# First weight tiles row by row through one queue, a position-bias table copied by ScalarE, and weights split four halves ahead

## The chip, the cores and the metric

The kernel runs on one core of one Trainium2 chip. The metric is the device time of one execution in microseconds (us), as the median of several runs.

The names used below: PE is TensorE (matmuls), ACT is ScalarE, DVE is VectorE, POOL is GpSimd, SP is SyncE, which here only issues DMAs. All weights and inputs are float32. A float32 operand is split into a part `hi`, rounded to the matmul format float32r, and the rest `lo`; a product is made from three matmuls (`hi*hi`, `hi*lo`, `lo*hi`, function `mm3`).

## The reference

A trunk of two layers over 256 positions and 2048 channels:

```python
h = x
for i in range(DEPTH):                       # DEPTH = 2
    hn = _rmsnorm(h, norm_g[i])
    u = hn @ w_in[i]                         # 2048 -> 5632 columns
    a_val, a_glu, a_z, q, k, v, b_z = jnp.split(u, offs, axis=-1)
    ya = _conformer_conv(a_val, a_glu, ...)  # GLU, depthwise conv of width 31, LayerNorm, SiLU
    ya = ya * jax.nn.silu(a_z)
    yb = _window_attention(q, k, v, bias_band, sink[i]) * jax.nn.silu(b_z)
    h = h + jnp.concatenate([ya, yb], axis=-1) @ w_out[i]
    e = _rmsnorm(p[i] @ w_pe[i], pe_g[i])
    h = h + e * jax.nn.sigmoid(h @ w_pg[i])
return _rmsnorm(h, final_g)
```

`bias_band` is a table of relative positions: for each head and each distance from -255 to 255 it holds `rel_bias[bucket(distance), head]`, or a very negative number beyond a distance of 128.

## The kernel before, in words

Everything is held transposed: channels on the 128 partitions, positions along the row. `x` is 16 slices (k = 0 to 15) of 128 channels by 256 positions. The weights lie in HBM as one stream in the order of use. Its unit is a *half*, 128x1024 numbers (512 KB), and two halves are a *chunk* of 1 MB, which is what one DMA normally brings (function `load`, line 166) into one of three buffers `raw`. ACT casts a half to `hi` (line 179) and DVE subtracts to get `lo` (line 180), both into one of five buffers `w`; this is `split`. `ahead(h)` splits up to half h, and `get(h)`, called when PE is to use half h, calls `ahead` first. PE, ACT and DVE work in the order of the program text (they are under a manual schedule); SP and POOL as the scheduler placed them. A row in a trace like `w<-raw` is such a cast or subtraction.

A HW DMA takes one of eight semaphores in turn, so the ninth waits for the first to have landed.

**The start.** Seven matmuls on zeros (`warm`, line 274) come first on PE. Then the first two of the eight column tiles of the GLU (value and gate each, so four 128-column groups) are computed from `x` that is not yet normalised, since the factor per position can be applied to the result: `firsts`, two PSUM banks, 16 slices x 4 groups x 3 matmuls = 192 matmuls named `ag`. For every slice ACT and DVE make `hg` (hi and lo of x times the gain, lines 563 and 564), ACT squares x (line 572, 8 operations of two slices), and DVE adds the squares into `sqs[0]` (lines 574 and 590). A half holds eight slices of one column group, and only the first 512 columns of four halves are needed for the first four slices; so the loads are cut into 256 KB parts (`load_part`, line 293), three of them issued by ACT and the rest by SP, and the work goes in four steps of four slices: split four parts, then 48 matmuls.

**The position embedding's product.** Then come four halves of `w_pe` (q = 0 to 3): `e = p @ w_pe`, 24 matmuls for each q in two groups of 12 (`epair`), whose results ACT copies out (line 519). Between them stands the norm's root: after q = 0, at the start of q = 1, PE sums the squares over partitions (`rh0c`, line 397), DVE makes the mean (`rh0v`, line 407), POOL takes the power -1/2 (`rh0col`, line 409), and PE turns the column into a row (`rh0b`, lines 416 and 418). ACT copies that row (line 422) and DVE scales the two banks of `firsts` by it (`ev`, line 600). The bank goes on to the sigmoid (`u`, line 637), the product (`az`) and the convolution on DVE (`cz`, line 623).

In before, `get(h)` for the first twelve halves of layer 0 splits two halves ahead of PE; from half 12 on it is `LS` = 4.

**The bias table.** `bias_prep` multiplies a one-hot table (33x511) by `rel_bias` on PE (`fps`, line 372), DVE copies the result (line 374) and POOL writes it to `fscr` in HBM. The attention reads its bands from there (`load_bias`).

After this the two layers go through their other tiles; the change leaves the code of those stages as it is.

Of the kernel before, what the change touches and what calls it, by code (L numbers as in the profile page):

```python
# [79 lines left out]
def weight_halves(l):  # L80
# [53 lines left out]

@with_exitstack
def trunk_kernel(ctx: ExitStack, tc: tile.TileContext, xT, pT, wst, par, gain, relb, sinkp, onehot, out):
# [24 lines left out]
    raws, spl, alone = {}, {}, {}  # L161
# [10 lines left out]
    def split_part(h, c):  # L172

        if h not in spl:
            w = wspl.tile([P, 2 * HALF + 64], F32R, tag="w", name=f"w{h}")
            spl[h] = w[:, SHIFT:SHIFT + 2 * HALF].rearrange("p (t n) -> p t n", t=2)
        raw = raws[h // 2][:, h % 2, c] if h // 2 in raws else alone[h][:, c]
        hi, lo = spl[h][:, 0, c], spl[h][:, 1, c]
        nc.scalar.copy(hi, raw)  # L179
        nc.vector.tensor_sub(lo, raw, hi.bitcast(F32))  # L180
# [100 lines left out]
    def load_part(h, n, eng=nc.sync, parts=2):  # L281

        c, x = h // 2, h % 2
        if h >= 6:
            if h not in alone:
                alone[h] = wk.tile([P, 4 * S + 32], F32, name=f"raw{h}alone", tag=f"qq{h % 2}", bufs=1)
            d = alone[h]
        else:
            if c not in raws:
                raws[c] = wraw.tile([P, 2, HALF], F32, tag="raw", name=f"raw{c}")  # L290
            d = raws[c][:, x, :]
        w = HALF // parts
        eng.dma_start(d[:, n * w:(n + 1) * w], wst[c, :, x * HALF + n * w:x * HALF + (n + 1) * w])

    def load_x(k, n=4, eng=nc.sync):
        eng.dma_start(h[k // 8][:, k % 8:k % 8 + n, :], xT[:, k:k + n, :])
# [6 lines left out]
    load_x(0, 1)  # L303
    nc.scalar.dma_start(gains, gain)
    load_x(1, 1)
    load_part(0, 0, nc.scalar)
    load_x(2, 2)
    load_part(1, 0, nc.scalar)
    load_part(2, 0, nc.scalar)
    junk = wk.tile([P, 2], F32, name="junk", tag="rv1", bufs=1)  # L310
    nc.scalar.activation(junk[:, 0:1], zeros[:, 0:1], AF.Copy, scale=2.0)
    load_part(3, 0)
    load_x(4)
    for x in range(4):
# [24 lines left out]
    relt = cst.tile([NUM_BUCKETS + 1, NQ], F32, name="relt")  # L339
    nc.vector.memset(relt[NUM_BUCKETS:NUM_BUCKETS + 1, :], NEG)  # L340
    oh = wk.tile([NUM_BUCKETS + 1, NREL], F32, name="oh", tag="sq", bufs=3)
    sinkt = cst.tile([P, DEPTH * NQ], F32, name="sinkt")

    def small_loads():
# [3 lines left out]
        nc.sync.dma_start(pf, pT[0])  # L348
        state["raw"] = 4
# [3 lines left out]
    def later_loads():  # L353

        for t in (oh[:, 0:1], sinkt[:, 0:1]):
            nc.vector.memset(t, 0.0)
        nc.sync.dma_start(relt[0:NUM_BUCKETS, :], relb)
        nc.sync.dma_start(oh, onehot)
# [10 lines left out]
    def bias_prep():  # L369
        nc.vector.tensor_scalar(nsink, sinkt, -1.0, None, ALU.mult)  # L370
        b = bank("fps").rearrange("p a b -> p (a b)")
        nc.tensor.matmul(b[0:NQ, 0:NREL], relt, oh, start=True, stop=True)
# [114 lines left out]
    for l in range(DEPTH):  # L487
# [65 lines left out]
        else:  # L553
            hg = [bigt(f"hg{l}_{i}", F32R) for i in range(2)]
            firsts = [bank(f"ag{l}_{t}") for t in range(2)]
            for n in range(4):
                c = slice((n % 2) * (HALF // 2), (n % 2 + 1) * (HALF // 2))
                ks = range(4 * n, 4 * n + 4)
                def part(k):

                    i, kk = k // 8, k % 8
                    hi, lo = (x[:, kk, :] for x in halves(hg[i]))
                    nc.scalar.activation(hi, h[i][:, kk, :], AF.Copy, scale=gcol(l, k))
                    nc.vector.scalar_tensor_tensor(lo, h[i][:, kk, :], gcol(l, k), hi.bitcast(F32),  # L564
                                                   ALU.mult, ALU.subtract)

                for y in range(4):
                    for k in ks[:1] if y == 0 else ks[1:] if y == 1 else []:
                        part(k)
                    split_part(4 * (n // 2) + y, c)  # L570
                for k in ks[::2]:
                    nc.scalar.activation(sqs[k // 2], h[k // 8][:, k % 8:k % 8 + 2, :], AF.Square)
                if n:
                    nc.vector.tensor_add(sqs[0], sqs[0], sqs[n])
                if n == 1:
                    small_loads()
                for y in range(4):
                    w = spl[4 * (n // 2) + y].rearrange("p t (k c) -> p t k c", k=8)
                    for k in ks:
                        mm3(firsts[y // 2][:, y % 2, :], w[:, :, k % 8, :], hg[k // 8][:, :, k % 8, :],  # L580
                            y % 2 == 0 and k == 0, k == KT - 1)
            for y in range(8):
                spl.pop(y)
# [4 lines left out]
            ahead(8)  # L588
            for x in range(4, 8):
                nc.vector.tensor_add(sqs[0], sqs[0], sqs[x])  # L590
            ahead(9)
# [60 lines left out]
        if l == 0:  # L652
            e = halves(bigt(f"e{l}"))
            eacc = wk.tile([P, 2, S], F32, name="eacc", tag="hacc")
            for q in range(4):
# [5 lines left out]
                if q == 2:  # L661
                    scaled = rstd_row(rcol, f"rh{l}", settle=2)
                    for t in range(2):
                        glu(t, firsts[t])
                for jj in range(0, 4, 2):
                    copied(4 * q + jj, epair(w, jj, pp))
                pump()

        def embed(l=l, eacc=eacc, e=e):

            if l == 0:
                yield from wait(4)
                bias_prep()
# [349 lines left out]
def buckets():  # L1023

    rel = np.arange(-(S - 1), S)
    half = NUM_BUCKETS // 2
    ret = (rel > 0).astype(np.int32) * half
    n = np.abs(rel)
    max_exact = half // 2
    large = max_exact + (np.log(np.maximum(n, 1) / max_exact) / np.log(MAX_DISTANCE / max_exact)  # L1030
                         * (half - max_exact)).astype(np.int32)
    large = np.minimum(large, half - 1)
    return ret + np.where(n < max_exact, n, large), n <= WINDOW


def band_onehot():
    b, band = buckets()
    m = np.zeros((NUM_BUCKETS + 1, NREL), np.float32)
    m[np.where(band, b, NUM_BUCKETS), np.arange(NREL)] = -1.0
    return np.ascontiguousarray(m[:, ::-1])  # L1040


# [5 lines left out]
def pack(inputs):  # L1048
# [17 lines left out]
    for l in range(DEPTH):  # L1066
# [31 lines left out]
```

## Time and profile before

| | |
|---|---|
| median of 3 runs | 932.85 us (932.72 to 933.32) |
| the profiled execution | 932.91 us; span from the first to the last instruction 931.1 us |
| PE busy | 920.1 us, 99% of the span |
| DVE busy | 773.9 us, 83% |
| ACT busy | 558.0 us, 60% |
| chain that ended last | PE 97%, ACT 1%, DVE 1%, DMA 1% |
| DMA | 182.55 MB, mean 196 GB/s |

A matmul's end is modelled in the profile, so two matmuls overlap in the rows, and a PE that is "busy" can still have lost a tenth of a microsecond between two starts. The time that PE lost is seen better in the distance from the start of one stage to the start of the next, compared with the number of matmuls between.

### The profile page before, as it was taken

The page shows a single profiled execution, that of the slowest core. Times are in us where ns is not written, and L with a number is a line of the kernel's source. Part 1 is how long each engine was busy: PE and PEld are TensorE (multiplying, and loading weights), DVE is VectorE, ACT ScalarE, POOL GpSimd, SP SyncE. Part 2 cuts the span into 40 slices and gives each one's busy share as a digit, 9 for nine tenths or more (in the row PEclk, how much of TensorE's full clock was granted, in tenths as well). Part 3 has the DMA queues.
Part 4 walks back from the last instruction along what each step waited for, and adds up shares of the span by engine and source line. Part 5 has one row for each costly group of instructions (what it writes and reads, how often), then busy time and mean ns, then how long its engine had stood idle before and what let it go on. Part 6 is the DMA issues. An engine that isn't in the chain of part 4 may idle for free.

```text
span 931.1 us, 19288 instructions
## 1 busy us (share of the span) xinstructions
PE 920.1 (99%) x8002; PEld 908.5 (98%) x8002; DVE 773.9 (83%) x1326; ACT 558.0 (60%) x853; POOL 59.4 (6%) x65
## 2 busy tenths in 40 slices
PE   9999999999999999999999999999999999999995
PEld 8999999999999999999999999999999999999995
DVE  7699999998998697786779998999888968777663
ACT  8744455688875475544466445568777556445551
POOL 0000101001000000011100000100100000000111
PEclk9999999999999999999999999999999999999998
DMA  9576546646455555556556555466454554655532
GB/s 338 204 250 222 188 176 207 209 167 206 170 193 220 182 226 181 182 184 260 190 185 224 187 221 182 182 221 215 157 178 170 198 210 152 234 184 182 207 108 90
DMA packets 30452, 182.55 MB, mean 196 GB/s; under 512 B 3756, under 2 KB 4573, under 8 KB 10653
## 3 DMA queue, kind: packets, MB, share of 16 engines
q1 hardware_dynamic: 25724, 166.46, 49.8%
q0 software_dynamic: 3344, 12.88, 4.1%
q10 hardware_dynamic: 1296, 1.99, 0.6%
q8 instruction: 62, 1.02, 0.4%
q14 instruction: 26, 0.20, 0.1%
HBM read 177.09 MB, written 4.23 MB: 195 GB/s over the span
## 4 chain that ended last, share of the span: by engine, by line
PE 97%; ACT 1%; DVE 1%; DMA 1%; issue 0%; SPq 0%; DVEq 0%; ACTq 0%
PE o L449 6%; PE o L450 6%; PE o L451 6%; PE g L451 6%; PE g L450 6%; PE g L449 6%; PE ag L451 6%; PE ag L450 6%; PE ag L449 6%; PE za L449 3%; PE za L450 3%; PE q L449 3%; PE za L451 3%; PE q L450 3%; PE q L451 3%; PE zb L449 3%
## 5 line engine op out<-in xcount | busy, mean ns | idle before, releaser
L180 DVE TENSOR_TENSOR w<-raw,w 128x1024 fp32r<-128x1024 f32 (+1 forms) x316 | 377.6, 1203 | 106.1 <-ACT w L179 104.9
L179 ACT CAST w<-raw 128x1024 fp32r<-128x1024 f32 (+1 forms) x316 | 319.0, 1030 | 178.2 <-PE o L451 38.8
L623 DVE SCALAR_TENSOR_TENSOR cz<-az,pars,cz 128x241 f32<-128x241 f32 (+14 forms) x480 | 202.9, 474 | 1.0 <-ACT cz L616 0.3
L451 PE MATMUL ag<-hg,w 128*128 128x256 f32 x512 | 141.6, 276 | 0.2 <-DVE w L180 0.2
L449 PE MATMUL ag<-hg,w 128*128 128x256 f32 x512 | 141.7, 277 | 0.0
L450 PE MATMUL ag<-hg,w 128*128 128x256 f32 x512 | 141.5, 276 | 0.1
L451 PE MATMUL g<-h,w 128*128 128x256 f32 x512 | 141.3, 276 | 0.0
L449 PE MATMUL g<-h,w 128*128 128x256 f32 x512 | 141.3, 276 | 0.0
L450 PE MATMUL g<-h,w 128*128 128x256 f32 x512 | 141.3, 276 | 0.0
L449 PEld LDWEIGHTS ag<-hg,w 128*128 128x128 f32 x512 | 96.1, 188 | 0.9 <-issue 0.8
L451 PEld LDWEIGHTS ag<-hg,w 128*128 128x128 f32 x512 | 96.1, 188 | 0.6 <-DVE w L180 0.6
L450 PEld LDWEIGHTS ag<-hg,w 128*128 128x128 f32 x512 | 96.1, 188 | 0.4 <-DVE hg L564 0.3
L449 PEld LDWEIGHTS g<-h,w 128*128 128x128 f32 x512 | 96.1, 188 | 0.0
L450 PEld LDWEIGHTS g<-h,w 128*128 128x128 f32 x512 | 96.1, 188 | 0.0
L451 PEld LDWEIGHTS g<-h,w 128*128 128x128 f32 x512 | 96.1, 188 | 0.0
L449 PE MATMUL o<-yb,w 128*128 128x256 f32 x256 | 71.8, 280 | 0.0
L449 PE MATMUL za<-hg,w 128*128 128x256 f32 x256 | 71.7, 280 | 0.0
L449 PE MATMUL q<-hg,w 128*128 128x256 f32 x256 | 71.4, 279 | 0.0
L449 PE MATMUL zb<-hg,w 128*128 128x256 f32 x256 | 71.3, 278 | 0.0
L450 PE MATMUL o<-yb,w 128*128 128x256 f32 x256 | 71.1, 278 | 0.0
L451 PE MATMUL o<-yb,w 128*128 128x256 f32 x256 | 71.1, 278 | 0.0
L451 PE MATMUL za<-hg,w 128*128 128x256 f32 x256 | 71.0, 277 | 0.0
(249 smaller groups left out, 2286.0 us busy)
## 6 DMA issues: line engine op xcount, KB each, us to landing
raw<-in_wst SPq DMA_DIRECT2D x152, 1024.0 KB, 4.8
bias<-fscr POOLq DMA_DIRECT2D x16, 384.0 KB, 3.9
raw<-in_wst SPq DMA_DIRECT2D x9, 256.0 KB, 7.0
az<-in_xT POOLq DMA_DIRECT2D x4, 512.0 KB, 5.3
hscr<-e POOLq DMA_DIRECT2D x2, 1024.0 KB, 6.7
az<-hscr POOLq DMA_DIRECT2D x4, 512.0 KB, 6.4
x<-in_xT SPq DMA_DIRECT2D x3, 512.0 KB, 6.8
out_t<-og ACTq DMA_DIRECT2D x4, 256.0 KB, 3.7
```

What stands on the lines that cost most here:

```text
L179: nc.scalar.copy(hi, raw)
L180: nc.vector.tensor_sub(lo, raw, hi.bitcast(F32))
L449: nc.tensor.matmul(o, w[:, 0], x[:, 0], start=start, stop=False, skip_group_check=True)
L450: nc.tensor.matmul(o, w[:, 0], x[:, 1], start=False, stop=False, skip_group_check=True)
L451: nc.tensor.matmul(o, w[:, 1], x[:, 0], start=False, stop=stop, skip_group_check=True)
L623: nc.vector.scalar_tensor_tensor(acc[:, t, lo_:hi_], a[:, t, lo_ + s:hi_ + s], w(k), acc[:, t, lo_:hi_], ALU.mult, ALU.add)
```

## The change

It has four parts, all in layer 0 before the first tile of normalised input:

1. **Rows.** The first eight halves hold two slices of all four column groups each, instead of eight slices of one. A quarter of a chunk (256 KB, a *row*) is what one slice needs. The loads (`load_rows`) and those of x go through SP alone, x and rows in turn; the last four rows come as one 1 MB DMA behind `p`, into the buffer that rows 0 to 3 had. The work goes in eight steps of two slices: operands, split, squares of the step before, 24 matmuls.
2. **Further ahead.** `get(h)` splits four halves ahead from the start; the halves of `w_pe` are then split earlier, and so are the first ones of tile 2. The norm's root row `rh0b` and what follows from it stand in the middle of q = 1, not at the end.
3. **The bias's table.** The one-hot, its load and the matmul go. `relb` is loaded transposed (16 heads on partitions, 32 buckets) by POOL at the start; the 511 places of the table are 33 runs of one bucket, two of them beyond the band. ACT writes 31 runs (`fs`, each a bucket's column broadcast, times -1), DVE sets the two others; two runs for each pump of the side work.
4. **Sigmoid first.** The first operation of ACT (`junk`) is a Sigmoid, not a Copy, so that its table is loaded at the start.

```diff
-    for ts in FIRST_TILES:
+    if l == 0:
+        cols = np.concatenate([off + tile_cols(t) for t in range(2) for off in (OFF_VAL, OFF_GLU)])
+        out += [("w_in", cols, k, 2) for k in range(0, KT, 2)] + W_PE
+    for ts in FIRST_TILES[l == 0:]:
...
+def bias_runs():
+    b, band = buckets()
+    v = [int(x) if y else None for x, y in zip(b[::-1], band[::-1])]
+    at = [n for n in range(NREL) if n == 0 or v[n] != v[n - 1]] + [NREL]
+    return [(x, y, v[x]) for x, y in zip(at, at[1:])]
...
     def get(h):
         r = h - NHALF
-        if h < 12:
-            ahead(h + 2)
-        elif 0 <= r < 12:
+        if 0 <= r < 12:
             ahead(h + (r | 1) + 2 - r)
         else:
             ahead(h + LS)
...
+    def load_rows(k, n=1):
+        c, w = k // 4, 2 * HALF // 4
+        if c not in raws:
+            raws[c] = wraw.tile([P, 2, HALF], F32, tag="raw", name=f"raw{c}")
+        x = (k % 4) * w
+        nc.sync.dma_start(raws[c].rearrange("p a b -> p (a b)")[:, x:x + n * w], wst[c, :, x:x + n * w])
...
+    for k in range(2):
+        load_x(k, 1)
+        load_rows(k)
+    for k in (2, 4, 6):
+        load_x(k, 2)
+        load_rows(k)
+        load_rows(k + 1)
+    load_x(8)
+    load_rows(8, 2)
+    load_rows(10, 2)
+    load_x(12)
     junk = wk.tile([P, 2], F32, name="junk", tag="rv1", bufs=1)
-    nc.scalar.activation(junk[:, 0:1], zeros[:, 0:1], AF.Copy, scale=2.0)
+    nc.scalar.activation(junk[:, 0:1], zeros[:, 0:1], AF.Sigmoid)
...
         nc.sync.dma_start(pf, pT[0])
+        load_rows(12, 4)
         state["raw"] = 4
         load(4)
...
     def bias_prep():
         nc.vector.tensor_scalar(nsink, sinkt, -1.0, None, ALU.mult)
-        b = bank("fps").rearrange("p a b -> p (a b)")
-        nc.tensor.matmul(b[0:NQ, 0:NREL], relt, oh, start=True, stop=True)
-        fs = wk.tile([NQ, NREL], F32, name="fs", tag="sq", bufs=3)
-        nc.vector.tensor_copy(fs, b[0:NQ, 0:NREL])
+        fs = wk.tile([P, 4 * S + 32], F32, name="fs", tag="qq0", bufs=1)[0:NQ, 0:NREL]
+        for n, (a, b, c) in enumerate(BIAS_RUNS):
+            if c is None:
+                nc.vector.memset(fs[:, a:b], -NEG)
+            else:
+                nc.scalar.mul(fs[:, a:b], relt[:, c:c + 1].broadcast_to([NQ, b - a]), -1.0)
+            if n % 2:
+                yield
...
+            for k in range(0, KT, 2):
+                part(k)
+                if k < 8:
+                    split_part(k // 2, slice(0, HALF // 2))
+                    part(k + 1)
+                    split_part(k // 2, slice(HALF // 2, HALF))
+                else:
+                    part(k + 1)
+                    split(k // 2)
+                if k:
+                    squares(k // 2 - 1)
+                if k == 4:
+                    small_loads()
+                w = spl.pop(k // 2).rearrange("p t (k y c) -> p t k y c", k=2, y=4)
+                for x in range(2):
+                    for y in range(4):
+                        mm3(firsts[y // 2][:, y % 2, :], w[:, :, x, y, :], hg[k // 8][:, :, (k + x) % 8, :], ...)
+            squares(7)
...
-            ahead(8)
-            for x in range(4, 8):
+            ahead(9)
+            for x in (1, 3, 5, 7):
                 nc.vector.tensor_add(sqs[0], sqs[0], sqs[x])
-            ahead(9)
+            ahead(10)
...
                 w = get(n).rearrange("p t (j k c) -> p t j k c", j=4, k=2)
-                if q == 2:
-                    scaled = rstd_row(rcol, f"rh{l}", settle=2)
-                    for t in range(2):
-                        glu(t, firsts[t])
                 for jj in range(0, 4, 2):
+                    if q == 1 and jj:
+                        scaled = rstd_row(rcol, f"rh{l}", settle=2)
+                        for t in range(2):
+                            glu(t, firsts[t])
                     copied(4 * q + jj, epair(w, jj, pp))
...
             if l == 0:
-                yield from wait(4)
-                bias_prep()
+                yield from bias_prep()
```

How the instructions stand shows three places. The first is DVE's queue around the norm's mean `rh0v`. In both, `w` is the subtraction of a half, `sqx` x4 are the last four sums of squares, `pp` is the lo part of p. Before:

```order
L484 TENSOR_TENSOR pp<-p_111,pp 128x512
L180 TENSOR_TENSOR w_463<-raw_267,w_463 128x1024
L590 TENSOR_TENSOR sqx<-sqx 128x512 x4
L180 TENSOR_TENSOR w_470<-raw_267,w_470 128x1024
L356 MEMSET oh 33x1
L356 MEMSET sinkt 128x1
L180 TENSOR_TENSOR w_485<-raw_459,w_485 128x1024
L407 TENSOR_SCALAR rh0v<-rh0c 128x2
L180 TENSOR_TENSOR w_525<-raw_459,w_525 128x1024
```

Now (line numbers of the changed kernel):

```order
L500 TENSOR_TENSOR pp<-p_111,pp 128x512
L205 TENSOR_TENSOR w_451<-raw_251,w_451 128x1024
L205 TENSOR_TENSOR w_454<-raw_251,w_454 128x1024
L612 TENSOR_TENSOR sqx<-sqx 128x512 x4
L205 TENSOR_TENSOR w_463<-raw_447,w_463 128x1024
L369 MEMSET sinkt 128x1
L205 TENSOR_TENSOR w_473<-raw_447,w_473 128x1024
L205 TENSOR_TENSOR w_478<-raw_449,w_478 128x1024
L423 TENSOR_SCALAR rh0v<-rh0c 128x2
L205 TENSOR_TENSOR w_518<-raw_449,w_518 128x1024
```

Five subtractions of whole halves stand ahead of `rh0v` where there were three, and two of them stand ahead of the sums of squares where there was one. The four rows of `w_pe` and the first half of tile 2 (`w_478`) are among them.

The second place is PE's queue around the root's row `rh0b`; `e` are the products of `w_pe`. Before, between the second group of q = 1 (`w_470`) and the first of q = 2:

```order
L451 MATMUL e<-pp,w_470 128x256
L416 MATMUL rh0b<-ident,rh0col 128x128 x2
L418 MATMUL rh0b<-ones 128x1 x2
L449 MATMUL e<-pp,w_485 128x256
L450 MATMUL e<-pp,w_485 128x256
```

Now, between the two groups of q = 1 (`w_454`):

```order
L467 MATMUL e<-pp,w_454 128x256
L432 MATMUL rh0b<-ident,rh0col 128x128 x2
L434 MATMUL rh0b<-ones 128x1 x2
L465 MATMUL e<-pp,w_454 128x256
L466 MATMUL e<-pp,w_454 128x256
```

From `rh0c` to `rh0b` there were 24 matmuls; now there are 12.

The third is SP's queue at the end of the first tiles' loads. Before, 256 KB parts, then `p`, then the chunk of `w_pe` (`raw_267`):

```order
L296 DMA x<-in_xT 128x1024
L293 DMA raw_130<-in_wst 128x512 x2
L293 DMA raw6alone<-in_wst 128x512
L293 DMA raw7alone<-in_wst 128x512
L348 DMA p_111<-in_pT 128x512
L166 DMA raw_267<-in_wst 128x2048
```

Now, with the last four rows (`raw_249`) behind `p`:

```order
L310 DMA raw_129<-in_wst 128x1024 x2
L313 DMA x<-in_xT 128x1024
L361 DMA p_111<-in_pT 128x512
L310 DMA raw_249<-in_wst 128x2048
L191 DMA raw_251<-in_wst 128x2048
```

The last operand of the first tiles lands behind `p` and as one piece of 1 MB, where before four parts of 256 KB came ahead of it.

More of the change, by code (lines that the diff above doesn't have):

```diff
@@ L132, with buckets, trunk_kernel @@
 PW = PO_PE + KT
+def buckets():
+    rel = np.arange(-(S - 1), S)
+    half = NUM_BUCKETS // 2
+    ret = (rel > 0).astype(np.int32) * half
+    n = np.abs(rel)
+    max_exact = half // 2
+    large = max_exact + (np.log(np.maximum(n, 1) / max_exact) / np.log(MAX_DISTANCE / max_exact)
+                         * (half - max_exact)).astype(np.int32)
+    large = np.minimum(large, half - 1)
+    return ret + np.where(n < max_exact, n, large), n <= WINDOW
+def bias_runs():
[3 more added lines that the diff above has]
+    return [(x, y, v[x]) for x, y in zip(at, at[1:])]
+BIAS_RUNS = bias_runs()
 @with_exitstack
-def trunk_kernel(ctx: ExitStack, tc: tile.TileContext, xT, pT, wst, par, gain, relb, sinkp, onehot, out):
+def trunk_kernel(ctx: ExitStack, tc: tile.TileContext, xT, pT, wst, par, gain, relb, sinkp, out):
     nc = tc.nc
@@ L279, in load_p, with load_x @@
         return pf
[L281 to L296, printed above, removed]
+    def load_rows(k, n=1):
[4 more added lines that the diff above has]
+        nc.sync.dma_start(raws[c].rearrange("p a b -> p (a b)")[:, x:x + n * w], wst[c, :, x:x + n * w])
+    def load_x(k, n=4):
+        nc.sync.dma_start(h[k // 8][:, k % 8:k % 8 + n, :], xT[:, k:k + n, :])
     h = halves(bigt("x"))
@@ L337, in trunk_kernel @@
     nc.vector.memset(mhalf, -0.5)
-    relt = cst.tile([NUM_BUCKETS + 1, NQ], F32, name="relt")
-    nc.vector.memset(relt[NUM_BUCKETS:NUM_BUCKETS + 1, :], NEG)
-    oh = wk.tile([NUM_BUCKETS + 1, NREL], F32, name="oh", tag="sq", bufs=3)
+    pad = cst.tile([P, NQ], F32, name="pad")
+    nc.gpsimd.memset(pad, 0.0)
+    relt = wk.tile([P, 4 * S + 32], F32, name="relt", tag="qq1", bufs=1)[0:NQ, 0:NUM_BUCKETS]
+    nc.gpsimd.dma_start(relt, relb)
     sinkt = cst.tile([P, DEPTH * NQ], F32, name="sinkt")
@@ L353, in later_loads @@
     def later_loads():
[L355 to L358, printed above, removed]
+        nc.vector.memset(sinkt[:, 0:1], 0.0)
         nc.sync.dma_start(sinkt, sinkp.partition_broadcast(P))
@@ L555, in trunk_kernel @@
             firsts = [bank(f"ag{l}_{t}") for t in range(2)]
[L556 to L575, printed above, removed]
-                    small_loads()
[L577 to L581, printed above, removed]
@@ L582, in trunk_kernel, with part, squares @@
-            for y in range(8):
-                spl.pop(y)
+            def part(k):
+                i, kk = k // 8, k % 8
+                hi, lo = (x[:, kk, :] for x in halves(hg[i]))
+                nc.scalar.activation(hi, h[i][:, kk, :], AF.Copy, scale=gcol(l, k))
+                nc.vector.scalar_tensor_tensor(lo, h[i][:, kk, :], gcol(l, k), hi.bitcast(F32),
+                                               ALU.mult, ALU.subtract)
+            def squares(x):
+                nc.scalar.activation(sqs[x], h[x // 4][:, 2 * x % 8:2 * x % 8 + 2, :], AF.Square)
+                if x % 2 == 0 and x:
+                    nc.vector.tensor_add(sqs[0], sqs[0], sqs[x])
@@ L1020, in trunk_kernel @@
             (nc.scalar if j >= 12 or j % 4 == 0 and x.start == 0 else nc.sync).dma_start(out[:, j:j + 2, :][:, x, :], d)
[L1023 to L1040, printed above, removed]
 def rows(v):
```

27 lines of the change are left out of this document (5 added, 22 removed).

## The prediction

> **What bounds the kernel now.** I read the page first (shares, chain), then PE's busy time by stage, then the first 45 us engine by engine, and last the chain at the few places where a stage took longer than its matmuls.
>
> ```profile
> PE 97%; ACT 1%; DVE 1%; DMA 1%; issue 0%; SPq 0%; DVEq 0%; ACTq 0%
> 0.00:6.45 6.45, 5.26 (x15) 4.28 (x15) 2.01 (x7) 2.91 (x5) 0.70 (x6) 1.00 0.67 212
> 6.45:9.11 2.66, 2.53 (x17) 2.12 (x16) 1.92 (x5) 2.42 (x6) 0.00 (x0) 1.00 1.00 320
> 9.11:29.19 20.08, 20.08 (x179) 20.08 (x178) 18.65 (x36) 18.69 (x37) 0.00 (x0) 1.00 1.00 388
> 41.68:53.02 11.34, 11.15 (x98) 10.96 (x97) 8.97 (x14) 8.89 (x12) 0.00 (x0) 1.00 0.55 186
> 53.02:65.08 12.06, 12.06 (x100) 11.08 (x99) 12.06 (x23) 4.41 (x5) 2.17 (x3) 1.00 0.58 190
> 65.08:75.96 10.88, 10.88 (x98) 10.88 (x97) 10.88 (x20) 4.41 (x5) 0.02 (x1) 1.00 0.76 276
> 75.96:917.90 841.94, 841.88 (x7371) 833.42 (x7369) 707.48 (x1206) 506.83 (x770) 52.60 (x52) 1.00 0.54 191
> ```
>
> The first row is the chain. The others cut the span where PE starts a stage (stretch, its length, then busy time of PE, PE's weight load, DVE, ACT and POOL, the granted clock, DMA share, GB/s). From 75.96 to 917.90 PE is busy throughout, and the code there stays, so nothing is to be won or lost behind 75.96 but by moving it as a whole. The three stretches from 41.68 on each hold the 96 matmuls of one GLU tile. The last of them is undisturbed: 10.88 us, or 0.1133 us for a matmul. The other two took 0.46 and 1.18 us longer. The first tiles' 192 matmuls fill 6.45 to 29.19, 22.74 us; at 0.1133 they would take 21.76. So PE loses 0.98 + 0.46 + 1.18 = 2.62 us in all where the change works. That is the most it can win, 0.28% of the time.
>
> In 9.11 to 29.19 DVE and ACT are busy 93% and the DMAs all the time. There is next to no slack on three engines at once, and this is where the change reorders work.
>
> ```profile
> 1.19 5.61 PE L274 MATMUL warm<-zeros 128*128 128x256 f32 x14 [1.19 <-DVE zeros L271]
> 6.45 0.47 PE L449 MATMUL ag<-hg,w 128*128 128x256 f32 x1
> 7.35 0.29 PE L449 MATMUL ag<-hg,w 128*128 128x256 f32 x1
> 7.78 0.38 PE L450 MATMUL ag<-hg,w 128*128 128x256 f32 x1
> 47.69 0.39 PE L451 MATMUL ag<-hg,w 128*128 128x256 f32 x1 [0.18 <-DVE w L180]
> 55.84 1.03 PE L372 MATMUL fps<-oh,relt 33*16 33x511 f32 x2
> ```
>
> The matmuls on zeros run until 6.45 in either kernel, so PE cannot start on x earlier. The losses are: waits for operands up to 9.11 (the step from 7.35 to 7.78 is the largest), one late split at 47.69, and the table's matmul at 55.84.
>
> **The change part by part.**
>
> *Gains.* The table's matmul goes: 1.18 us, all on PE's path. The split at 47.69 belongs to tile 2, whose halves were cast two ahead and behind a table load on ACT; with four ahead the first of them is split before `rh0b`. I take the full 0.46 (bounds 0 and 0.46). For the first matmuls, slice 0 now needs one x slice and one row, 384 KB, where the first step needed 1.5 MB for its 48 matmuls; I take 0.98 (bounds 0 and 0.98), subject to the next paragraph.
>
> *Costs hidden.*
>
> ```profile
> 166.52 0.19 ACT L784 ACTIVATE es<-es 128x4 f32<-128x4 f32 x1
> 63.62 1.48 POOL L382 DMA_DIRECT2D bias<-fscr  x2 [1.90 <-DMA fscr<-fs]
> 158.21 0.95 PE sc L769 x8
> 39.76 1.28 ACT L637 ACT_TABLE_LOAD   x1
> ```
>
> The 31 copies of the bias table: the nearest row, a small ACT operation, took 0.19 us, so 6 us, spread over 16 pumps while ACT is busy 4.41 of 10.88 us in a tile. They hide; without that cover they would cost those 6 us. The table was fetched back at 63.62 and is needed only when the attention's scores are ready, behind 158; that it is written some tiles later costs nothing. The Sigmoid at the start takes the place of a load there, and the load at 39.76 (1.28 us of ACT) goes; ACT's time there is no bound of PE but through the late split, counted above.
>
> *The cost that is not hidden: `rh0b`.* PE's order puts the root's row 12 matmuls behind `rh0c`, and the DVE puts `rh0v` behind five whole subtractions. So the question is when DVE gets through its queue, and that hangs on the landing of the last rows, 12 to 15, since everything behind is in order.
>
> ```profile
> 0.00:12.90 12.90, 11.58 (x63) 10.19 (x64) 6.89 (x17) 9.03 (x18) 0.70 (x6) 1.00 0.84 288
> 0.00:20.10 20.10, 18.78 (x126) 17.39 (x127) 14.06 (x32) 16.23 (x33) 0.70 (x6) 1.00 0.92 327
> 1.66:10.50 8.84, 8.71 (x42) 7.32 (x42) 4.36 (x8) 6.72 (x13) 0.00 (x0) 1.00 0.95 307
> 10.50:18.00 7.50, 7.50 (x69) 7.50 (x68) 7.11 (x17) 7.41 (x17) 0.00 (x0) 1.00 1.05 403
> 7.06 0.54 SPq L296 DMA_DIRECT2D x<-in_xT  x1
> p<-in_pT SPq DMA_DIRECT2D x1, 256.0 KB, 6.9
> 15.69 0.33 SPq L348 DMA_DIRECT2D p<-in_pT  x1
> DMA to landing us min/median/max: 6.9/6.9/6.9
> ```
>
> Up to and with rows 12 to 15 the same bytes go in both kernels as before up to `p`: gains 25, x 2097, weights 4194, p 262, together 6578 kB. Before, 327 GB/s x 20.1 us = 6573 kB had been taken up by 20.1. Landing comes later: the x slices issued at 7.06 landed 6.9 us on, at 13.97, and they were the 3695th kB, taken up by 12.9 (288 x 12.9 = 3715). That is 1.1 us. So the rows land at 20.1 + 1.1 = 21.2. The upper end is p's own landing, 15.69 + 6.9 = 22.6, which lies behind the same bytes. The lower end takes the rate of 10.5 to 18.0 from the start: 1.66 + 6578/403 + 1.1 = 19.1. I take 21.2: the bytes and the engines that move them are the same, and no row says that one queue starts faster than two.
>
> Ahead of that the tightest is slice 8: its rows, up to the 4219th kB, land at 13.97 + (4219 - 3695)/403 = 15.3, and by the rows below are cast 1.05 and subtracted 1.23 later, at 17.6. PE wants the lo part at 6.45 + 98 x 0.1133 = 17.55. I count no loss there; one would be swallowed by the wait that follows.
>
> ```profile
> 20.68 1.31 ACT L563 ACTIVATE hg<-x,gains 128x256 fp32r<-128x256 f32 x3
> 23.44 1.15 ACT L572 ACTIVATE sqx<-x 128x512 f32<-128x512 f32 x2
> 24.49 0.60 ACT L483 CAST pp<-p 128x512 fp32r<-128x512 f32 x1
> 25.19 2.00 ACT L179 CAST w<-raw 128x1024 fp32r<-128x1024 f32 x2
> 27.41 2.86 DVE L590 TENSOR_TENSOR sqx<-sqx 128x512 f32<-128x512 f32 x4
> 30.19 2.37 DVE L180 TENSOR_TENSOR w<-raw,w 128x1024 fp32r<-128x1024 f32 x2
> 32.90 0.16 DVE L407 TENSOR_SCALAR rh0v<-rh0c 128x2 f32<-128x2 f32 x1 [0.34 <-PE rh0c L397]
> 33.14 0.70 POOL L409 TENSOR_TENSOR rh0col<-rh0v,mhalf 128x2 f32<-128x2 f32 x1 [31.84 <-DVE rh0v L407]
> 46.41 3.50 DVE L180 TENSOR_TENSOR w<-raw,w 128x1024 fp32r<-128x1024 f32 x3 [0.96 <-ACT w L179]
> 32.08 0.79 PE rh0c L397 x8
> 35.55 0.38 PE L416 MATMUL rh0b<-ident,rh0col 128*128 128x128 f32 x2
> ```
>
> From the landing on, ACT has in order: cast of slices 12 and 13 (0.95 from start to start, by the row of two that took 2.00), squares 0.53, two `hg` 0.81, cast of 14 and 15 0.95, two squares 1.05, pp 0.60, cast of the first `w_pe` half 1.05: 5.94 us, to 27.2. Then DVE: two subtractions 2.28 (2.37 less the overlap), four sums of squares 2.78, three subtractions 3.42, `rh0v` 0.16; POOL 0.08 + 0.70; 0.06 to PE: 9.48, so `rh0b` starts at 36.7.
>
> Without waits PE would stand there at 6.45 + 216 x 0.1133 + 0.79 + 12 x 0.1133 = 33.1; it waits some 3.6 us in all (at slice 12, at `rh0c` and most of it at `rh0b`). Before, `rh0b` was at 35.55 behind 12 more matmuls (1.36), so the same point lay at 34.2. PE is there 36.7 - 34.2 = 2.5 us later, the 0.98 included. What is late next is only what follows `rh0b` on ACT and DVE, and PE has 72 matmuls of `w_pe` and tile 2's first halves, split already, to cover it.
>
> The sum: +2.5 - 0.46 - 1.18 = +0.9 us on the profiled execution's 932.91 (0.06 above the median of the runs), so 933.8.
>
> A general rule of the time: 932.91 + (landing of rows 12 to 15 - 20.3).
>
> The Trainium skill (DMA: Bandwidth & Descriptors, Rules for kernel authors) says that spreading DMAs over issuing engines brings no bandwidth, since all run on the same 16 engines; by that, giving up ACT's three issues neither hurts nor helps, and the landing stays at 21.2. The trace's 307 GB/s with two queues agrees as far as it shows.
>
> **The rivals.**
>
> *The rows come late (slower).* If 12 to 15 land when p did, at 22.6, slice 12 is split at 22.6 + 2.3 = 24.9 where PE wants it at 6.45 + 146 x 0.1133 = 23.0, PE already waits 1.9 there, and by the rule above the sum is 932.91 + 2.3 = 935.2. It decides from a landing of 22.2 on. For it speaks that the last transfer is one piece that must land whole; against it, that p landed 2.5 us behind the time at which its bytes had been taken up (20.1), where the x slices took 1.1.
>
> *DVE does not decide (faster).* If `rh0v` came in time, all three losses would go: 932.91 - 2.62 = 930.3. That needs `rh0b` at 33.1, a landing by 17.6; by 18.4 the gain would be just over 0.2%. For it speaks only that DVE's and ACT's operations might overlap better than I add them. Against it: 18.4 needs 6578 kB in 18.4 - 1.1 - 1.66 = 15.6 us, 420 GB/s from the first packet on, more than any stretch above.
>
> *The rows come early, no change either.* With 403 GB/s throughout the landing is 19.1 and the time 931.7.
>
> *The clock falls.* PE waits 2 to 2.5 us in one piece at `rh0b`.
>
> ```profile
> 2.63 3.95 PE L274 MATMUL warm<-zeros 128*128 128x256 f32 x10
> 5.62 0.97 PE L274 MATMUL warm<-zeros 128*128 128x256 f32 x3
> ```
>
> The passes on zeros ran slowly at first: seven from 2.63 to 5.62, 0.427 us each, then three until 6.45, 0.28 each and still falling. Were PE thrown back to half its pace for as long as there (1.19 to 5.62), half of 4.4 us would be lost: 933.8 + 2.2 = 936.0. Against it: the granted clock is 1.00 in every stretch above, though none of them has such a wait, so the trace doesn't settle it. The Trainium skill (TensorE: Matmul & The Clock Gate, What's actually happening) puts the fall after an idle window of about 3.4 us; by it a wait of 2.5 us is too short and this rival falls.
>
> **How the numbers follow.** A measurement of this kernel can tell about 0.2% (1.9 us) from no change. Landing between 20 and 22.1: 0.58, time 932.6 to 934.7. Early rows: 0.10. Late rows: 0.17; clock 0.05; together with a small rest for an unseen cost, slower by over 0.2% is 0.24. DVE not deciding: 0.08, which is all of faster. No change: 0.68. The likeliest gives 933.8. The range reaches from the early rows to the late ones, 931.7 to 935.3, the bounds of the landing; above lies the clock, below the case without a wait.
>
> **What would show it.** Right: no wait of PE before slice 8 or so; a wait of about 2 us before `rh0b` with POOL's `rh0col` as its releaser and `rh0v` straight behind a subtraction; rows 12 to 15 landing near 21; no `fps` and no wait near 47; tile 3 to the end at the pace of before. Wrong: `rh0b` without a wait, or waits of PE in the first eight slices, or a granted clock below 1.0 near 36.

## The result, and the profile after

The changed kernel takes 938.85 us (median of 6 runs, 937.67 to 941.42) against 933.28 (932.72 to 933.40): a ratio of 1.0064, 95% interval 1.0052 to 1.0076. It is 5.6 us slower. The forecast was 933.8, range 931.7 to 935.3.

The profiled execution took 937.99 us, 5.1 more than that of before. Its chain, then PE's stages as in the prediction: first tiles, `w_pe` up to `rh0b`, from there to tile 2, tiles 2 and 3, the rest (stretch, its length, busy time of PE, weight load, DVE, ACT, POOL, granted clock, DMA share, GB/s).

```profile
PE 92%; DVE 3%; DMA 2%; ACT 1%; issue 1%; SPq 0%; POOL 0%; DVEq 0%; ACTq 0%
6.45:31.18 24.73, 23.33 (x194) 22.51 (x193) 19.67 (x34) 21.37 (x38) 0.00 (x0) 1.00 0.91 349
31.18:39.55 8.37, 5.53 (x46) 5.13 (x44) 7.63 (x11) 4.34 (x6) 1.63 (x1) 1.00 0.63 232
39.55:48.70 9.15, 9.14 (x66) 9.15 (x67) 3.66 (x6) 5.25 (x10) 0.00 (x0) 0.81 0.41 172
48.70:59.58 10.88, 10.88 (x98) 10.88 (x97) 10.47 (x20) 6.20 (x14) 0.00 (x0) 1.00 0.58 194
59.58:70.46 10.88, 10.88 (x98) 10.88 (x97) 10.79 (x20) 5.39 (x13) 0.00 (x0) 1.00 0.52 194
70.46:922.77 852.31, 852.11 (x7464) 844.01 (x7462) 715.65 (x1218) 513.73 (x791) 51.59 (x55) 1.00 0.54 191
```

Tiles 2 and 3 now take 10.88 each: the 0.46 and 1.18 us are gone, as forecast. The first tiles take 24.73, not 22.74. In the second row PE is busy 5.53 of 8.37. The third has a granted clock of 0.81. PE's waits up to 48 us (us in total, times, longest):

```profile
PE rh0b L432 <- POOL rh0col L425: 2.7, 1, 2.7
PE ag L467 <- DVE w L205: 1.4, 3, 0.7
PE rh0c L413 <- DVE sqx L612: 0.2, 1, 0.2
```

The instructions around the longest of them, and the issue of rows 12 to 15, in the timeline:

```profile
36.62 0.28 PE L467 MATMUL e<-pp,w 128*128 128x256 f32 x1
39.55 0.43 PE L432 MATMUL rh0b<-ident,rh0col 128*128 128x128 f32 x2 [2.66 <-POOL rh0col L425]
37.63 0.15 DVE L423 TENSOR_SCALAR rh0v<-rh0c 128x2 f32<-128x2 f32 x1
37.70 1.22 DVE L205 TENSOR_TENSOR w<-raw,w 128x1024 fp32r<-128x1024 f32 x1
37.87 1.63 POOL L425 TENSOR_TENSOR rh0col<-rh0v,mhalf 128x2 f32<-128x2 f32 x1 [35.44 <-DVE rh0v L423]
14.50 0.38 SPq L310 DMA_DIRECT2D raw<-in_wst  x1
```

That transfer's size and time from issue to landing:

```profile
raw<-in_wst SPq DMA_DIRECT2D x1, 1024.0 KB, 8.7
```

Two stretches of 3.41 us on either side of 40.06, in the same columns as the stages:

```profile
36.65:40.06 3.41, 0.75 (x8) 0.55 (x7) 2.27 (x3) 0.59 (x1) 1.63 (x1) 1.00 0.60 228
40.06:43.47 3.41, 3.41 (x18) 3.41 (x18) 1.29 (x2) 0.58 (x2) 0.00 (x0) 0.50 0.95 394
```

PE starts no matmul between 36.62 and 39.55. (A wait at `rh0b` is given in this document as this distance from start to start, 2.9 here; the idle time in the rows, 2.66, is shorter because the modelled end of a matmul lies later than the next start would.) `rh0v` ends at 37.78, behind the subtractions, and then the power takes POOL 1.63 us, not 0.70, while DVE subtracts the next half. The rows 12 to 15 (issue at 14.50) land 8.7 later, at 23.20. And in the window behind the wait the clock is 0.50: 18 matmuls where some 30 fit at 0.1133.

From start to start PE is later by 1.99 at the end of the first tiles, 2.44 at `rh0c`, 5.36 at `rh0b` (39.55 against 34.19, which is before's 35.55 less twelve matmuls), then +1.67 (clock), -0.46, -1.18: 5.39 at the end of tile 3, of which 0.3 come back later. The runs of after lie 3.7 us apart, those of before 0.7. The runs below show in part where that is from.

### The profile page after: what moved, and what is told of

It is laid out like the page before. It is cut to its first block, busy times and chain, and to the rows that moved or that the text cites. A ratio compares the mean times of both kernels' runs of the same rounds, so it can differ in the third digit from the quotient of the medians.

```text
span 936.2 us, 19295 instructions
## 1 busy us (share of the span) xinstructions
PE 921.2 (98%) x8000; PEld 910.3 (97%) x8000; DVE 774.6 (83%) x1321; ACT 560.9 (60%) x879; POOL 57.9 (6%) x67
## 4 chain that ended last, share of the span: by engine, by line
PE 92%; DVE 3%; DMA 2%; ACT 1%; issue 1%; SPq 0%; POOL 0%; DVEq 0%; ACTq 0%
PE o L465 6%; PE o L466 6%; PE g L465 6%; PE o L467 6%; PE g L467 6%; PE g L466 6%; PE ag L465 5%; PE ag L467 5%; PE ag L466 5%; PE za L465 3%; PE za L467 3%; PE za L466 3%; PE q L465 3%; PE q L466 3%; PE q L467 3%; PE zb L465 3%
```

## The experiments

All are compared with runs of before on the same chip (medians 932.6 to 933.3).

### The wait, and the clock behind it

**PE work where PE waited** (`idle_fill`):

```diff
+NIDLE = 12
...
                     if q == 1 and jj:
+                        idle(NIDLE)
                         scaled = rstd_row(rcol, f"rh{l}", settle=2)
```

> The kernel after, with 12 idle matmuls (128x128, on the bank idle, not used by anything) in PE's order straight ahead of rh0b; they add about 12 x 0.21 = 2.6 us of PE work where PE waits 2.9. Theory (the idle wait itself makes the clock fall): rh0b stays at 39.5 to 39.8, the granted clock stays at 1.0, and 1.7 us of the slow stretch go: 936.3 against 938.0 of the profiled execution, and the runs lie close together. Rival (the clock falls for another reason, a limit on power or the matmuls of w_pe): the slow stretch stays, 938 or more.

936.74 us (936.54 to 937.23, 4 runs). The same two stretches of time as above:

```profile
36.65:40.06 3.41, 3.41 (x31) 3.27 (x30) 2.64 (x4) 0.59 (x1) 1.63 (x1) 1.00 0.68 187
40.06:43.47 3.41, 3.41 (x31) 3.41 (x31) 1.29 (x2) 1.62 (x5) 0.00 (x0) 1.00 1.02 428
```

31 matmuls in place of 18: work that nobody needs makes the kernel 2.1 us faster in the median. Against the profiled run of after, 937.99, it is 1.3, where 1.7 were expected. So the wait makes the clock fall. The four runs also lie close together, but `q2_fill` below shows that a filled wait does not bring that by itself.

**`rh0b` back to q == 2** (`row_q2`):

```diff
-                    if q == 1 and jj:
+                    if q == 2 and not jj:
                         scaled = rstd_row(rcol, f"rh{l}", settle=2)
```

> The kernel after, with rh0b (and the GLU evictions behind it) put back to the start of step q == 2, so that PE has 12 more matmuls of w_pe ahead of it. Theory (PE's wait at rh0b, and the clock that falls behind it, make most of the loss): rh0b starts at 39.5 as before, since DVE decides, but PE reaches it at 36.6 + 1.4 = 38.0, waits 1.6 instead of 2.9, and the granted clock stays at 1.0: 1.4 + 1.7 = 3.0 us less, 935.0. If the clock falls in spite of the shorter wait: 936.6. Rival (the clock falls for another reason, and the place of rh0b does not matter): 938 to 941 as after.

938.06 us (934.59 to 938.86, 5 runs). `rh0b` at 39.13 behind a wait of 1.58 and no fall of the clock, as expected, but only one run came near the 935.0. The others are 2.8 to 4.3 us above that one, though nothing waits behind `rh0b`. The stretch from 60 to 100 us tells why (x is the count of matmuls). Before:

```profile
60.00:100.00 40.00, 40.00 (x356) 40.00 (x355) 40.00 (x75) 17.71 (x21) 4.40 (x4) 1.00 0.60 218
```

row_q2:

```profile
60.00:100.00 40.00, 40.00 (x342) 40.00 (x341) 37.79 (x69) 19.60 (x42) 2.26 (x4) 1.00 0.53 193
```

PE is busy all of it at clock 1.00, and does 342 matmuls, not 356. From start to start they are 117.8 ns apart, where the forecast counted every matmul at 113.3. The slower pace runs from `rh0b` to 136 us and costs 97 x 4.5/117.8 = 3.7 us. It was there to be seen in before's trace, behind the stages that the prediction shows: the products `o<-yb` from 290 to 300 us are 117.8 ns apart too.

### The steps that make `rh0b` late

**The split behind `rh0v` moved behind `rh0b`** (`split_behind`):

```diff
-                w = get(n).rearrange(...)
+                w = (spl.pop(n) if q == 1 else get(n)).rearrange(...)
...
                         scaled = rstd_row(rcol, f"rh{l}", settle=2)
+                        ahead(n + LS)
```

> The kernel after, with the split that get() does in step q == 1 put behind rh0b, so that DVE has no subtraction to run while POOL works on rh0col. Theory (POOL's pow takes 1.63 us only because a DVE subtraction runs beside it): pow takes 0.70 as in the kernel before, rh0b starts at 38.6 instead of 39.5, PE waits 2.0. Without a fall of the clock 935.4; each run in which PE comes out of the wait at the slower pace of 117.8 ns takes up to 3.7 more. Rival (the pow is slow for another reason): 1.6 us, rh0b at 39.5, 938 to 941.

937.63 us (936.85 to 939.56, 4 runs). The timeline there:

```profile
37.67 0.15 DVE L423 TENSOR_SCALAR rh0v<-rh0c 128x2 f32<-128x2 f32 x1
37.91 0.72 POOL L425 TENSOR_TENSOR rh0col<-rh0v,mhalf 128x2 f32<-128x2 f32 x1 [35.47 <-DVE rh0v L423]
38.68 0.43 PE L432 MATMUL rh0b<-ident,rh0col 128*128 128x128 f32 x2 [1.72 <-POOL rh0col L425]
```

The stretch with the wait, and the one behind it:

```profile
36.22:39.64 3.42, 1.70 (x16) 1.49 (x14) 1.60 (x3) 0.73 (x2) 0.72 (x1) 1.00 0.52 177
39.64:43.05 3.41, 3.41 (x19) 3.41 (x18) 2.21 (x3) 2.10 (x4) 0.00 (x0) 0.50 0.34 144
```

With DVE quiet the power takes 0.72, and `rh0b` is where it was expected, 38.68. But behind a wait of 2.0 us the clock still fell in the profiled run, and all runs lie above the 935.4.

**Two halves ahead, as before** (`two_ahead`):

```diff
+        if h < 12:
+            ahead(h + 2)
-        if 0 <= r < 12:
+        elif 0 <= r < 12:
```

> The kernel after, with weights split two halves ahead up to half 11, as before: rh0v then stands behind one w_pe half less two (halves 11 and 12 come behind it) on DVE. Theory (rh0v behind these subtractions makes the wait): rh0v at 35.3 instead of 37.6, rh0b at 36.6 to 37.3, PE waits under 0.8 there, the clock stays at 1.0 and the time is 938.0 - 2.3 - 1.7 = 934.0, up to 0.5 more if the late split near 47 comes back. Rival (the wait is made by the late landing alone): rh0b still at 39 or later, 938.

936.07 us (933.67 to 938.78, 10 runs). In the profiled run `rh0v` is at 35.60, the power takes 1.63 again (a subtraction starts at 35.67), `rh0b` is at 37.52 behind a wait of 0.72, the clock stays at 1.0: all as expected, and the fastest runs are near the 934.0. The others reach 938.8; by their times they have the slower pace, but the profiled run (934.6) is one of the fast ones, so no trace shows it.

**Both undone** (`two_ahead_q2`: the two edits above together):

> The kernel after with both part 2 undone (weights two halves ahead up to half 11) and rh0b back at the start of step q == 2: of the change, the rows, the single queue, the Sigmoid and the bias copies are left. Theory: PE reaches rh0b at 36.8 + 1.4 = 38.2, behind rh0col's end at 37.5, so there is no wait, no fall of the clock and no slower pace: 934.6 (the profiled run of two_ahead) - 0.7 = 933.9, in all runs. It is still not faster than before, since the first tiles end 2.0 us later. Rival (a slower pace or a fall of the clock whatever PE waits): 936 to 938.

935.40 us (933.12 to 937.50, 10 runs). No wait at `rh0b` and no fall of the clock; half of the runs at 933.1 to 934.8, the others at 936.0 to 937.5. The profiled run (937.5) is of the slower pace from `rh0b` to 136 us. So the mechanism of the wait holds, and "in all runs" does not.

### The landing

**Two issuing engines** (`two_queues`):

```diff
     for k in range(2):
         load_x(k, 1)
-        load_rows(k)
+        load_rows(k, 1, nc.scalar)
...
+    load_rows(2, 1, nc.scalar)
```

> The kernel after, with rows 0, 1 and 2 issued by ACT behind its gains, as before three pieces were, so that the first transfers are issued from two engines side by side; everything else stays. Theory A (one issuing engine, 0.45 us an issue, starves the DMAs up to 4.5 us and so makes rows 12 to 15 land 2.0 us late): they land at 21.2 to 22, rh0b comes 1.2 to 2 us earlier, PE waits 1 to 1.7 there, the clock may hold: 934.5 to 937. Rival B (the relative bias's load by POOL, or the pieces in flight, slow the start): rows 12 to 15 land at 23.2 as after and the time stays at 938 to 939.

938.84 us (935.34 to 940.12, 5 runs). The first 14 us (last column GB/s) before:

```profile
0.00:14.00 14.00, 12.68 (x72) 11.29 (x73) 7.99 (x19) 10.13 (x21) 0.70 (x6) 1.00 0.86 296
```

After:

```profile
0.00:14.00 14.00, 12.54 (x72) 11.13 (x72) 6.93 (x17) 8.98 (x17) 1.47 (x8) 1.00 0.75 250
```

two_queues:

```profile
0.00:14.00 14.00, 12.38 (x77) 11.02 (x78) 7.45 (x18) 9.43 (x19) 1.47 (x8) 1.00 0.85 289
```

Its issue of rows 12 to 15 is at 13.81, and to the landing it takes:

```profile
raw<-in_wst SPq DMA_DIRECT2D x1, 1024.0 KB, 9.5
```

A second issuing engine brings the early rate back (289 of 296 GB/s), yet the rows land at 23.3, as in after, and `rh0b` stays at 39.66. Theory A is wrong on the landing. B's numbers came, but this run does not test the causes that B names. The Trainium skill (DMA: Bandwidth & Descriptors, Rules for kernel authors) says that a second issuing engine saves only issue time. The early rate was 16% higher with it here, in one profile each, while the landing agrees with the rule.

**Rows 12 to 15 in two pieces ahead of p** (`rows_first`, on two_ahead_q2):

```diff
-        nc.sync.dma_start(pf, pT[0])
-        load_rows(12, 4)
+        load_rows(12, 2)
+        load_rows(14, 2)
+        nc.sync.dma_start(pf, pT[0])
```

> two_ahead_q2 with rows 12 to 15 issued in two pieces ahead of p instead of in one behind it. Theory (PE's last waits in the first tiles, at slices 8 and 12, come from that piece's landing at 23.2): rows 12 and 13 land near 21.3, rows 14 and 15 near 22.6, the wait of 1.0 us at slice 12 goes, and the first tiles end about 1 us earlier: 932.9. Rival (DVE and ACT set the first tiles' end, not the landing): within 0.3 us of two_ahead_q2.

932.95 us (931.84 to 935.22, 10 runs). That is the time of before (ratio 0.9996, 0.9987 to 1.0006): what is left of the change costs nothing and wins nothing. The pieces landed at 22.5 and 23.8, a microsecond later than expected, but the first one still ahead of the old piece, and that sufficed: the wait at slice 12 is gone. PE's waits up to 48 us in two_ahead_q2:

```profile
PE ag L469 <- DVE w L205: 1.2, 3, 0.8
PE rh0c L415 <- DVE sqx L614: 0.5, 1, 0.5
PE ag L467 <- ACT w L204: 0.4, 2, 0.2
```

In rows_first:

```profile
PE ag L470 <- DVE w L205: 0.6, 3, 0.2
PE ag L468 <- ACT w L204: 0.5, 1, 0.5
```

Against the faster half of two_ahead_q2 it is about 0.9 us. The rest of the 2.4 is, as far as the times tell, that most of its runs kept the pace of 113.3 behind `rh0b`, as the profiled one did.

### What decides the pace

**A filled wait in row_q2** (`q2_fill`: `idle(8)` ahead of `rh0b`):

> row_q2 with 8 idle matmuls (1.7 us of PE work on a bank not used) straight ahead of rh0b, where PE waited 1.6 us. Theory (a wait ahead of rh0b, not the place of it, makes PE come out at 117.8 ns a matmul instead of 113.3 until the next small matmuls at 136 us, 3.7 us in all): the pace behind rh0b is 113.3, the time is the fastest run of row_q2, 934.6, and 0.1 more, in all of its runs: added work makes the kernel faster than row_q2's 938.1. Rival (the slower pace comes from the place of rh0b among the matmuls): 938 again.

938.53 us (937.76 to 938.82, 4 runs). No wait at `rh0b` (39.55, straight behind the idle matmuls), the slower pace in the profiled run, and no run below 937.7. The theory is refuted: the wait makes the clock fall, but it does not set the pace.

**Two one-column matmuls behind `w_pe`** (`q2_kick` on row_q2, `after_kick` on after):

```diff
+            kick = bank("kick0")
+            for b in range(2):
+                nc.tensor.matmul(kick[:, 0, b:b + 1], ones, ones[:, 0:1], start=True, stop=True, ...)
```

> row_q2 with two matmuls of one column (on a bank not used) behind the last matmul of w_pe, some 3 us behind rh0b, as the kernel has them behind v at 136 us, where PE went back to 113.3 ns a matmul in every trace. Theory (what row_q2 loses against its own fastest run is the pace of 117.8 ns from rh0b to 136 us and nothing else, and such matmuls, issued without a wait ahead of them, clear it): all runs at 934.6 + 0.4 for the two matmuls = 935.0, against a median of 938.1. Rival (the slower pace is set by what runs on the other engines there, and comes back): 938.5.

> The kernel after with the same two matmuls behind the last of w_pe. Theory: the runs of after near 941.4 are those that have both the fall of the clock and the slower pace; with the pace cleared they go, and what is left lies between 936.7 (no fall) and 938.4 (fall). Rival: runs at 940 and above stay.

q2_kick: 938.14 us (938.03 to 939.43, 4 runs), at 117.8 ns ahead of the two matmuls and behind them. after_kick: 942.64 us (938.92 to 944.48, 4 runs); in its profiled run the clock stayed at 0.5 for two windows (39.66 to 46.48) and the slower pace came behind that. Both theories fell.

**Four instead of two small matmuls behind the transposes** (`q2_settle4`: `settle=4`):

> row_q2 with four instead of two one-column matmuls straight behind the transposes of rh0b. If the number of them behind rh0b decides at which pace PE goes on, the runs gather at one value, 934.8 or 938.5; if it is the time at which the wait ahead of rh0b ends, they stay mixed as in row_q2 (934.6 to 938.9).

937.70 us (936.17 to 939.35, 4 runs): mixed, so the number of small matmuls does not decide the pace. Its profile has the shortest wait behind which the clock fell, 1.49 us (row_q2 kept 1.00 behind 1.58):

```profile
37.10:40.51 3.41, 2.20 (x20) 1.99 (x19) 2.22 (x3) 2.00 (x3) 1.47 (x1) 1.00 0.80 327
40.51:43.92 3.41, 3.41 (x19) 3.41 (x18) 1.09 (x2) 0.59 (x1) 0.00 (x0) 0.50 0.63 255
```

**The layout alone** (`shift64`, `shift128`, on before):

```diff
+    pad = cst.tile([P, 16], F32, name="pad")      # 32 columns in shift128
+    nc.gpsimd.memset(pad, 0.0)
     relt = cst.tile([NUM_BUCKETS + 1, NQ], F32, name="relt")
```

> The kernel before with one constant of 64 bytes a partition, filled once by POOL and not used, ahead of relt, so that everything behind it in SBUF moves by 64 bytes; no instruction of the path changes. If the place in SBUF alone set PE's slower pace in bias_only (117.8 ns a matmul from 364 to 473 us and from 767 to 928): 933.3 + 3.9 + 6.1 = 943.3. If not: 933.3.

> The same with 128 bytes. If only the alignment to 128 bytes matters: 933.3, beside 943.3 for shift64. If any move brings another pace: other than 933.3, between 930 and 945. If the place does not matter: 933.3 in both.

shift64: 945.88 us (943.82 to 947.14, 4 runs), ratio 1.0130 (1.0116 to 1.0145). shift128: 950.25 us (948.08 to 952.80, 4 runs), ratio 1.0188 (1.0172 to 1.0205). The stretch from 780 to 820 us before:

```profile
780.00:820.00 40.00, 40.00 (x355) 40.00 (x354) 29.89 (x34) 21.16 (x25) 0.00 (x0) 1.00 0.59 211
```

shift64:

```profile
780.00:820.00 40.00, 40.00 (x342) 40.00 (x341) 30.62 (x36) 21.05 (x26) 0.00 (x0) 1.00 0.56 196
```

shift128:

```profile
780.00:820.00 40.00, 40.00 (x342) 40.00 (x342) 29.24 (x34) 21.21 (x27) 0.00 (x0) 1.00 0.52 185
```

342 matmuls in place of 355 again, over long stretches of both: 64 bytes that no instruction of the path uses cost 1.3%. shift64 lies near the 943.3 expected if the place alone sets the pace; shift128 lies above every number expected of it. The kernel after keeps the layout of the constants by its text (its `pad` stands where `relt` stood), so a moved constant is not what sets the pace in after.

### The bias table and the Sigmoid by themselves

**The copies** (`bias_only`; `bias_pad`, with the constants' place kept), **the Sigmoid** (`sig_only`), **both** (`best1` = bias_pad and Sigmoid), all on before. Beside the change's `bias_prep`:

```diff
-    relt = cst.tile([NUM_BUCKETS + 1, NQ], F32, name="relt")
+    relt = cst.tile([NQ, NUM_BUCKETS], F32, name="relt")                       # bias_only
+    pad = cst.tile([P, NQ], F32, name="pad")                                   # bias_pad, best1
+    relt = wk.tile([P, 2, S], F32, name="relt", tag="sq", bufs=3)[0:NQ, 0, 0:NUM_BUCKETS]
...
-    nc.scalar.activation(junk[:, 0:1], zeros[:, 0:1], AF.Copy, scale=2.0)
+    nc.scalar.activation(junk[:, 0:1], zeros[:, 0:1], AF.Sigmoid)              # sig_only, best1
```

> The kernel before with only the bias table's part: no one-hot matrix, the table copied run by run by ACT (relt loaded later by SP, as before). Theory: the matmul fps (1.18 us of PE's path) goes and the copies hide: 933.3 - 1.2 = 932.1. Rival (the 31 copies delay ACT's casts): 933.3 or more.

> The kernel before with the bias table copied run by run by ACT, as in bias_only, but with the constants' place in SBUF as before: relt lies in the slot of the one-hot matrix, and 64 bytes of padding stand where it lay (in bias_only it was 128 bytes and moved everything behind it by 64). Theory (the copies are hidden, and what bias_only lost is PE's slower pace of 117.8 ns a matmul from 364 to 473 us and from 767 to 928 us, far from the change): the pace stays at 113.3 ns there, only fps goes: 933.1 - 1.2 = 931.9. Rival (the copies cost it): 943 again.

> The kernel before with the junk activation at the start a Sigmoid and nothing else. bias_pad took PE's 1.2 us out of the GLU stages and gave them back at the transposes pt near 174 us, where PE waited for ACT and DVE; best1, with the Sigmoid, kept them. Theory (DVE, 100% busy from 76 to 108 us, sets when the first pt can start, and the table load at 39.76 delays DVE's first convolutions by 1.3 us): the late split at 47.69 goes and the wait at pt shrinks: 933.3 - 0.5 to 0.8 = 932.5 to 932.8, and pt does not wait. Rival (the Sigmoid alone is what best1 gained): 931.7.

> bias_pad with the junk activation at the start a Sigmoid, so that ACT's table load at 39.76 goes. If the late split at 47.69 in the second GLU stage came from that load, 0.46 us more go: 931.4. If not, 931.9 as bias_pad.

| | median, us | runs | ratio and interval |
|---|---|---|---|
| bias_only | 943.37 | 4 | 1.0110 (1.0095 to 1.0125) |
| bias_pad | 933.34 | 11 | 1.0000 (0.9991 to 1.0009) |
| sig_only | 932.49 | 11 | 0.9992 (0.9983 to 1.0001) |
| best1 | 931.68 | 11 | 0.9982 (0.9973 to 0.9991) |

bias_only's loss was the layout: bias_pad, with the same copies, does not have it. But the 1.2 us that bias_pad was to win did not come: in its profile PE is 0.5 us earlier than before at `k` (108.11 against 108.60) and 0.3 later at the first transposes of the attention, `pt` (173.91 against 173.57). bias_pad from 76 to 108 us (third busy time: DVE):

```profile
76.00:108.00 32.00, 32.00 (x285) 32.00 (x284) 32.00 (x59) 14.90 (x25) 3.83 (x4) 1.00 0.69 239
```

PE's wait at `pt` in bias_pad (before has none there):

```profile
PE pt L822 <- ACT s L816: 1.0, 2, 0.7
```

And in best1:

```profile
PE pt L822 <- ACT s L816: 0.3, 1, 0.3
```

DVE is busy without a gap there, and what it delivers for `pt` does not come earlier because PE does. With the Sigmoid, ACT's table load at 39.76 goes, DVE begins its convolutions at 43.16 and not at 44.98, and the 1.2 us hold: best1 is 1.6 us faster than before, close to the 931.4 expected. sig_only came at its 932.5, but its interval reaches 1.0001, so by itself it is not clear of no change. In bias_pad's profile the first tiles were also 1.3 us longer than in before, and DVE began its convolutions 0.7 later; how much of that is chance, and so how much of the wait at `pt`, stays open.

## Why the prediction was wrong

- **Gains.** The table's matmul (1.18) and the late split (0.46) went as worked out, and the copies hid. The late split came from the table load: in sig_only, which splits two halves ahead, tile 2 takes 10.88 too. But "nothing is to be won or lost behind 75.96 but by moving it as a whole" did not hold for bias_pad, which in its profile lost behind 75.96 what it had won, with DVE as a second bound, and in the median won nothing. In after this does not show: there DVE's convolutions begin 2.7 later than before and PE reaches `k` 5.4 later. The 0.98 of the first tiles did not come: they were 1.99 longer.
- **The landing of rows 12 to 15: the mis-sized term.** 21.2 forecast, upper bound 22.6, measured 23.20. The start was slower: up to 21.4 the mean was 308 GB/s, so the 6578 kB were in at 21.4, not 20.1. And the piece was whole 1.8 later, not 1.1. The 1.1 was the lag of the x slices; `p`, behind the same bytes in before, had landed 2.5 after they were in, and the forecast used that row for its bound only. The count of bytes gives no landing, since transfers issued later are under way by then: at 23.20, 317 GB/s had moved 7354 kB, 776 more than the 6578. The same lateness showed earlier: rows 8 and 9 landed at 16.86, not 15.3, and PE lost 0.6 at slice 8. "No row says that one queue starts faster than two" was true of before's trace; two_queues shows the rate rise and the landing stay. rows_first shows that the piece and its place behind p cost about 0.9 us. By the forecast's own rule the measured landing would have given 932.91 + 2.9 = 935.8, so it is not the whole of the miss.
- **From the landing to `rh0b`.** 15.5 forecast, 16.35 measured. The sum took POOL's power at 0.70 from a row where DVE was idle for most of it; beside a subtraction it takes 1.63 (split_behind: 0.72 again). The order printed in the description shows that subtraction straight behind `rh0v`. The Trainium skill (SBUF — State Buffer, SBUF: two separate sides) says that a DVE operation with two SBUF inputs and a GpSimd operation lock the same pair of ports for a whole instruction; the 1.63 agrees: the power ended 0.58 behind the subtraction that had started ahead of it. The prediction should have used it.
- **The clock.** A rival at 0.05, priced at 2.2 us: it came, at 1.67 in the profiled run, and it held in split_behind with 2.0 us of wait. What was argued against it, that a wait of 2 to 2.5 us is too short, was wrong.
- **One pace.** All terms were matmuls at 0.1133. Variants of after go on at 0.1178 from `rh0b` to 136 us in part of the cases, 3.7 us. That would explain the runs of after at 941.4 (938.0 + 3.7 = 941.7) as far as their times show. A second window at half clock, as in after_kick, would add 1.7 (939.7; one run took 939.62). The profiled run had one such window and the faster pace behind it, so neither is seen in a trace of after.

0.9 forecast + 2.0 (landing) + 0.85 (power and the steps around it) + 1.67 (clock) = 5.4, as measured at the end of tile 3. The mechanism, the root's mean queued behind subtractions with too little PE work ahead of it, was right (two_ahead); the sizes were not, and the clock was left out of the sum. Of the rivals, "the rows come late" and "the clock falls" came true together.

## What to carry to other kernels

A wait of PE has two prices, its length and what PE does when it comes out of it. Here 2.9 us of wait cost 1.7 more by the clock, and idle matmuls in it were a gain. For the landing of a transfer, use the row whose transfer stands where yours will stand. When PE is 99% busy, look which engine is at 100% in the stages behind before counting a gain as kept, and move constants in SBUF only with a run that shows what the move does by itself.

## What the runs showed of the hardware

- **The clock's window.** The granted clock changes at steps of 3.41 us that don't start with the wait. A window in which PE loaded no weights for 2.9 (after), 1.9 (split_behind) or 1.4 us (q2_settle4) of it was followed by 0.50; row_q2 and q2_kick had 1.5 and 1.4 in a window and kept 1.00, and two_queues kept it through a wait of 2.91 that lay across two windows with 1.4 and 1.5. So the edge lies near 1.4 to 1.5 us, and idle time alone does not place it: what else counts is not shown. The Trainium skill (TensorE: Matmul & The Clock Gate, What's actually happening) has the same free-running window, 3413 ns, but asks for a whole idle one; here less than half sufficed.
- **Two paces of PE.** 113.3 and 117.8 ns for a float32r matmul of 256 columns, at a granted clock of 1.00, each kept from some ten to over a hundred microseconds; a few short rows ran at 120 (shift64, `e<-pp` at 482 to 483 us). In before and in after the pace changed only where small matmuls or a wait break the row (after had 117.8 from 26 to 35 us too). With a constant moved it also changed in an unbroken row, where the operands change: in shift128 from 113.3 to 117.8 at 466.67, where `g<-h` ends and `e<-pp` begins. Moving what lies behind one constant by 64 bytes brought the slower pace over 270 us and more (bias_only, shift64: all 8 runs at least 9.5 us longer). So the place of the operands counts. What sets the pace at `rh0b` is open: neither a wait ahead of it nor two small matmuls behind it decide it. That the timing at that place does was not shown.
- **POOL beside DVE.** A power of 128x2 takes POOL 0.70 to 0.72 us alone and 1.63 when a DVE subtraction of 128x1024 starts just ahead of it.
